# The taps of a depthwise convolution: VectorE alone, or shared with ScalarE and GpSimd

## The chip, the core and the metric

One core of a Trainium2 chip runs the whole program. The metric is device time in microseconds (us), the median over several executions. The engines are TensorE (PE for its matmuls, PEld for its weight loads), VectorE (DVE), ScalarE (ACT), GpSimd (POOL) and SyncE (SP, which issues DMAs). Each works through its own queue in order; semaphores tie the queues together.

## The reference

The program is a chain of three transformer-like blocks on x of 1024 positions by 1024 channels in float32. The change lies in the third block, whose input projection gives, among others, two halves of 512 channels for a gated convolution:

```python
def conformer_conv(glu_a, glu_b, dw_w, dw_b, cln_g, cln_b, pw_w, pw_b):
    u = glu_a * jax.nn.sigmoid(glu_b)
    pad = CONV_WIDTH // 2                       # CONV_WIDTH = 31
    u = lax.conv_general_dilated(
        u, dw_w[:, None, :].astype(u.dtype), window_strides=(1,),
        padding=[(pad, pad)], dimension_numbers=("NWC", "WIO", "NWC"),
        feature_group_count=u.shape[-1]) + dw_b
    u = layer_norm(u, cln_g, cln_b)
    u = jax.nn.silu(u)
    return u @ pw_w + pw_b
```

Each channel is convolved with its own 31 weights ("taps") along the 1024 positions. Beside this branch, the block computes a neighbourhood attention of 8 heads from the same projection. Both branches are normalised by groups, gated, joined and multiplied with w_out; a last norm gives the output.

## The kernel before

Activations lie with channels on the 128 partitions, so the 512 convolved channels are four tiles (i = 0 to 3) of 128 channels by 1024 positions. Each projection is a sum of matmuls in which every float32 operand is split into a rounded part "hi" and a remainder "lo": `weight` (lines 78 to 88) loads 128x1024 weights, makes `w_hi` on ScalarE or VectorE, and `w_lo` by a subtraction on GpSimd (line 87). Matmul results go to PSUM tiles of few buffers: `mm` has 2, `mf` has 1.

`block3` starts at line 1268. `glu(i)` (line 1283) makes the gated tile `u` of 128 x 1054 in a pool with two buffers for `u`; per half of 512 positions ScalarE takes a tanh (line 1290), and VectorE finishes the sigmoid (line 1291) and multiplies (line 1292). `dwconv(i, u)` (line 1297) then adds up 31 taps. Tap 0 is a multiply and add of the bias on VectorE (line 1304). Taps 1 to 20 are each one VectorE instruction, accumulator `cy` = `u` shifted by k, times a weight, plus `cy` (line 1306). Taps 21 to 30 go another way: ScalarE multiplies the shifted `u` by the weight, the first into `y2` (line 1308), the other nine one after the other into `pr`, a tile with one buffer (line 1311), and GpSimd adds each `pr` to `y2` (line 1312). The trace calls the tile `y2` "y". Last, VectorE adds `y2` to `cy` (line 1313) and SyncE stores `cy` to the DRAM tile `cv_d` (line 1314).

The order: convolutions 0 and 1 are emitted first (`convs`, lines 1425 to 1432). The attention runs in four pairs of heads, `na_pair(0)` to `na_pair(3)` (line 1370), each with projections split into `qs`, `ks`, `kl` (lines 144, 268, 273 and 279) and eight attention steps (`attend_steps`). One step goes PE scores, VectorE bias and maximum (line 329), ScalarE exponential (line 335), VectorE reciprocal and scaling (lines 337 and 341), PE transposes (line 346), ScalarE and VectorE split (lines 137 and 139), PE product (line 359), ScalarE copy (line 361), VectorE sum (line 366). `weave` (line 192) mixes other work between the steps: convolutions 2 and 3 and one gate projection in pair 0 (line 1437); `conv_ln` and `conv_pw` of one half in pair 1 and of the other in pair 2. `conv_ln` reads `cv_d` back (line 1321), transposes it (line 1324) and normalises it, so it needs all four convolutions.

The program is not run in the order in which it is written: the Tile layer's scheduler orders each engine's queue beforehand by its own timeline, in which an instruction that was emitted earlier goes first among those that are ready.

Of the kernel before, what the change touches and what calls it, by code (L numbers as in the profile page):

```python
# [10 lines left out]
F32 = mybir.dt.float32  # L11
F32R = mybir.dt.float32r
AF = mybir.ActivationFunctionType
ALU = mybir.AluOpType
# [4 lines left out]
P = 128  # L19
S = 1024  # L20
# [11 lines left out]
def kernel(ctx: ExitStack, tc: tile.TileContext, a, out, blocks=(1, 2, 3)):  # L32
    nc = tc.nc
    mm = nc.tensor.matmul
    act = nc.scalar.activation
    stt = nc.vector.scalar_tensor_tensor
    tt = nc.vector.tensor_tensor
    ts = nc.vector.tensor_scalar

    def pool(name, bufs=1, space=None, side=None, c=ctx):  # L40
        kw = {} if space is None else {"space": space}
        if side:
            kw["side"] = side
        if space is not DRAM:
            kw["reuse_waits"] = "tile"
        return c.enter_context(tc.tile_pool(name=name, bufs=bufs, **kw))
# [25 lines left out]
    def col(name, i, src=None):  # L72
        o = COL[name] + i
        return (cols if src is None else src)[:, o:o + 1]
# [1193 lines left out]
    def block3(x3, begin, finish):  # L1268
        x_st, x_fm = x3
        w3 = a["w_in_3"]  # L1270
        TAP, PAD = 31, 15
        POOL_TAPS = 10
        nc.scalar.dma_start(rpb_d.rearrange("r (b k) -> r b k", k=16),
                            bass.AP(tensor=a["rpb"].tensor, offset=a["rpb"].offset,
                                    ap=[[1, 16], [32, 248], [1, 16]]))
# [5 lines left out]
        cp = pool("conv", side="right", c=us)  # L1281
# [14 lines left out]

        def dwconv(i, u):
            y = cp.tile([P, S], F32, name="cy", tag="cy", bufs=2)
            y2 = cp.tile([P, S], F32, name="y2", tag="y2")
            for k in range(TAP):  # L1300
                w = col("dw_w_3", 4 * k + i)
                src = u[:, k:k + S]
                if k == 0:
                    ts(out=y, in0=src, scalar1=w, scalar2=col("dw_b_3", i), op0=ALU.mult, op1=ALU.add)
                elif k < TAP - POOL_TAPS:
                    stt(out=y, in0=src, scalar=w, in1=y, op0=ALU.mult, op1=ALU.add)  # L1306
                elif k == TAP - POOL_TAPS:
                    act(out=y2, in_=src, func=AF.Copy, scale=w)
                else:
                    pr = cp.tile([P, S], F32, name="pr", tag="pr", bufs=1)  # L1310
                    act(out=pr, in_=src, func=AF.Copy, scale=w)
                    nc.gpsimd.tensor_tensor(out=y2, in0=y2, in1=pr, op=ALU.add)
            tt(out=y, in0=y, in1=y2, op=ALU.add)
            nc.sync.dma_start(cv_d[i], y)

        def conv_ln(cp2, n_fm, hf):
# [104 lines left out]
        def conv_in(i):  # L1421
            u = yield from glu(i)
            dwconv(i, u)
# [85 lines left out]
    for b, body in ((1, block1), (2, block2), (3, block3)):  # L1509
        if b not in blocks:  # L1510
            continue
        n = b + 1 if b + 1 in blocks else 4
        if nxt is None:
            nxt = a["x"] if b == 1 else start(begin[b](), finish[b])
        nxt = body(nxt, begin[n], finish[n])
# [111 lines left out]
```

## Time and profile before

| | |
|---|---|
| Median of 3 runs | 3456.34 us (3452.67 to 3456.74) |
| The profiled execution, its own time | 3451.47 us |
| Its span, first to last instruction | 3449.7 us |
| Mean granted clock of TensorE | 0.971 |
| Third block's convolutions, taps on VectorE | 2828.8 to 3067 us of the span |

The page's first part gives the busy time of each engine. The chain of waits follows the work that ended last back through what released it. The window view gives busy time by engine for a stretch; the grouped view gives count, total and mean of like instructions; the timeline shows single instructions, where "x2" joins two neighbours and a bracket gives the idle time before one with its releaser. VectorE's instructions overlap by a few hundredths of a microsecond at their borders, so an instruction of 1.28 us takes 1.20 us from start to start.

### The profile page before, as it was taken

What the parts mean: (1) busy time and instruction counts of PE and PEld (TensorE: products, weight loads), DVE (VectorE), ACT (ScalarE), POOL (GpSimd) and SP (SyncE); (2) the same over time, 40 slices, a digit from 0 to 9 for tenths busy, and PEclk for the clock granted to TensorE, in tenths of its full rate; (3) what the DMA queues carried; (4) which work ended last, traced back from release to release, by engine and by line L of the source; (5) the groups of instructions that cost most, each with busy time, mean ns of one, the idle gap of its engine ahead of it and who ended that gap; (6) DMA issues with size and microseconds to landing.
All of it is one profiled execution on the core that took longest, in us unless ns stands there. A gap on an engine that the chain in (4) does not pass through costs nothing. (4 is left out here: it accounts for less than half of the span.)

```text
span 3449.7 us, 39897 instructions
## 1 busy us (share of the span) xinstructions
PE 3247.2 (94%) x14976; PEld 2658.2 (77%) x14976; DVE 2082.8 (60%) x3220; ACT 1102.8 (32%) x2038; POOL 1480.4 (43%) x949
## 2 busy tenths in 40 slices
PE   7999999999999999999978998999999986889998
PEld 6888888877888788778767776888888865667776
DVE  5455556374454455557768857444455679985665
ACT  3333311033223310311244532233321133445552
POOL 3111122266555642134434358555564456552221
PEclk9999999999999999999989999999999998989999
DMA  4211125212222432222251021222243221122241
GB/s 140 66 61 53 62 68 171 67 46 74 83 83 83 147 98 74 75 89 89 90 182 56 25 86 56 82 83 83 83 152 98 76 75 43 46 89 78 78 147 68
DMA packets 107474, 293.34 MB, mean 85 GB/s; under 512 B 15232, under 2 KB 20608, under 8 KB 107280
## 3 DMA queue, kind: packets, MB, share of 16 engines
q1 hardware_dynamic: 79184, 240.75, 21.4%
q10 hardware_dynamic: 28096, 50.04, 4.4%
q8 instruction: 118, 1.93, 0.2%
q14 instruction: 76, 0.62, 0.1%
HBM read 227.24 MB, written 63.76 MB: 84 GB/s over the span
## 5 line engine op out<-in xcount | busy, mean ns | idle before, releaser
L87 POOL TENSOR_TENSOR w_lo<-w_raw,w_hi 128x1024 fp32r<-128x1024 f32 x187 | 470.3, 2520 | 1042.4 <-DVE w_hi L86 569.2
L95 PE MATMUL mm<-x,w_hi 128*128 128x512 f32 x688 | 279.6, 407 | 22.9 <-DVE qs L144 10.8
L96 PE MATMUL mm<-x,w_hi 128*128 128x512 f32 x688 | 279.6, 406 | 0.0
L97 PE MATMUL mm<-x,w_lo 128*128 128x512 f32 x688 | 275.7, 402 | 1.0 <-POOL w_lo L87 1.0
L438 POOL TENSOR_TENSOR w_lo<-s,w_hi 128x512 fp32r<-128x512 f32 x160 | 220.2, 1384 | 103.9 <-ACT w_hi L437 102.5
L95 PE MATMUL mf<-x,w_hi 128*128 128x512 f32 x576 | 233.5, 405 | 17.9 <-DVE u L1292 13.9
L97 PE MATMUL mf<-x,w_lo 128*128 128x512 f32 x576 | 229.2, 398 | 1.2 <-POOL w_lo L87 1.2
L96 PE MATMUL mf<-x,w_hi 128*128 128x512 f32 x576 | 229.9, 399 | 0.0
L565 DVE TENSOR_TENSOR h<-h,mm 128x512 f32<-128x512 f32 x214 | 146.7, 687 | 134.7 <-PE mm L97 134.6
L438 POOL TENSOR_TENSOR w_lo<-w_raw,w_hi 128x512 fp32r<-128x512 f32 x120 | 172.1, 1434 | 97.7 <-ACT w_hi L437 97.4
L86 DVE CAST w_hi<-w_raw 128x1024 fp32r<-128x1024 f32 x143 | 134.9, 944 | 128.3 <-PE mm L96 58.6
L519 DVE TENSOR_TENSOR u<-p,pb 128x512 f32<-128x512 f32 x40 | 27.5, 687 | 248.6 <-PE pb L97 248.6
L95 PEld LDWEIGHTS mm<-x,w_hi 128*128 128x128 f32 x688 | 132.6, 193 | 55.7 <-issue 23.4
L437 ACT CAST w_hi<-s 128x512 fp32r<-128x512 f32 x160 | 97.2, 619 | 243.3 <-PE pc L96 148.6
L1306 DVE SCALAR_TENSOR_TENSOR cy<-u,cols,cy 128x1024 f32<-128x1024 f32 x80 | 166.2, 2084 | 0.9
L97 PEld LDWEIGHTS mm<-x,w_lo 128*128 128x128 f32 x688 | 132.5, 193 | 30.4 <-issue 2.2
L96 PEld LDWEIGHTS mm<-x,w_hi 128*128 128x128 f32 x688 | 133.1, 193 | 27.4 <-issue 2.1
L335 ACT ACTIVATE st<-st,nmax 128x128 f32<-128x128 f32 (+5 forms) x192 | 119.3, 623 | 107.2 <-DVE nmax L329 101.4
L95 PE MATMUL mm<-w_hi,act 128*128 128x512 f32 x384 | 150.5, 392 | 2.9 <-DVE h L565 2.9
L96 PE MATMUL mm<-w_lo,act 128*128 128x512 f32 x384 | 150.5, 392 | 0.3 <-POOL w_lo L87 0.3
L97 PE MATMUL mm<-w_hi,act 128*128 128x512 f32 x384 | 150.3, 392 | 0.0
L95 PEld LDWEIGHTS mf<-x,w_hi 128*128 128x128 f32 x576 | 110.7, 192 | 42.2 <-DVE u L1292 15.0
(505 smaller groups left out, 9017.4 us busy)
## 6 DMA issues: line engine op xcount, KB each, us to landing
w_raw<-in_w_ffn_in_dram SPq DMA_DIRECT2D x88, 512.0 KB, 3.6
w_raw<-in_w_in_dram SPq DMA_DIRECT2D x78, 512.0 KB, 3.7
act_d<-ao SPq DMA_DIRECT2D x88, 256.0 KB, 2.0
w_raw<-in_w_ffn_out_dram SPq DMA_DIRECT2D x44, 512.0 KB, 3.9
act<-act_d SPq DMA_DIRECT2D x36, 512.0 KB, 4.3
w_raw<-in_w_out_dram SPq DMA_DIRECT2D x24, 512.0 KB, 3.7
gates_d<-go SPq DMA_DIRECT2D x32, 256.0 KB, 2.0
gt<-gates_d ACTq DMA_DIRECT2D x32, 256.0 KB, 3.4
```

Source lines behind the costliest of these rows:

```text
L86: nc.vector.tensor_copy(hi, raw)
L87: nc.gpsimd.tensor_tensor(out=lo, in0=raw, in1=f(hi), op=ALU.subtract)
L95: mm(out_, lh, rh, start=start and i == 0, stop=False, **kw)
L96: mm(out_, lh, rl, start=False, stop=False, **kw)
L97: mm(out_, ll, rh, start=False, stop=stop and i == n - 1, **kw)
L335: act(out=st[:, :w + extra], in_=st[:, :w + extra], func=AF.Exp, scale=-1.0, bias=nmax, accum_out=ssum)
L437: nc.scalar.copy(hi, src)
L438: eng(out=lo, in0=src, in1=f(hi), op=ALU.subtract)
L519: tt(out=u3, in0=p1, in1=pb, op=ALU.add)
L565: tt(out=hh, in0=hh, in1=pt, op=ALU.add)
L1306: stt(out=y, in0=src, scalar=w, in1=y, op0=ALU.mult, op1=ALU.add)
```

## The change

All 31 taps are computed by VectorE's multiply-add of line 1306. The ten ScalarE multiplications of a tile, the nine GpSimd additions, the closing VectorE addition and the tiles `y2` and `pr` are gone. Everything else in the program text is the same; the scheduler orders the queues anew.

```diff
-        POOL_TAPS = 10
...
         def dwconv(i, u):
             y = cp.tile([P, S], F32, name="cy", tag="cy", bufs=2)
-            y2 = cp.tile([P, S], F32, name="y2", tag="y2")
             for k in range(TAP):
                 w = col("dw_w_3", 4 * k + i)
                 src = u[:, k:k + S]
                 if k == 0:
                     ts(out=y, in0=src, scalar1=w, scalar2=col("dw_b_3", i), op0=ALU.mult, op1=ALU.add)
-                elif k < TAP - POOL_TAPS:
+                else:
                     stt(out=y, in0=src, scalar=w, in1=y, op0=ALU.mult, op1=ALU.add)
-                elif k == TAP - POOL_TAPS:
-                    act(out=y2, in_=src, func=AF.Copy, scale=w)
-                else:
-                    pr = cp.tile([P, S], F32, name="pr", tag="pr", bufs=1)
-                    act(out=pr, in_=src, func=AF.Copy, scale=w)
-                    nc.gpsimd.tensor_tensor(out=y2, in0=y2, in1=pr, op=ALU.add)
-            tt(out=y, in0=y, in1=y2, op=ALU.add)
             nc.sync.dma_start(cv_d[i], y)
```

## Rows read from the trace of the kernel before

**Rows 1.** Page: busy us of each engine, share of the span, instructions

```profile
PE 3247.2 (94%) x14976; PEld 2658.2 (77%) x14976; DVE 2082.8 (60%) x3220; ACT 1102.8 (32%) x2038; POOL 1480.4 (43%) x949
```

**Rows 2.** Windows: stretch, its us, busy us of each engine, granted clock, DMA

```profile
2828.80:3067.00 238.20, 190.69 (x789) 147.04 (x788) 236.48 (x227) 95.37 (x143) 142.60 (x59) 0.88 0.15 45
3067.00:3092.00 25.00, 19.93 (x77) 15.03 (x76) 17.93 (x22) 11.51 (x21) 14.78 (x6) 0.80 0.30 95
3092.00:3449.70 357.70, 330.01 (x1467) 255.31 (x1465) 210.65 (x445) 169.20 (x330) 75.85 (x49) 0.95 0.28 97
```

**Rows 3.** Chain of waits, 2828 to 3092 us: start, us, what (its longest pieces)

```profile
2943.39 3.32 DVE cy L1306
2947.04 3.33 DVE cy L1306
...
3070.59 4.64 DVE gr L1260 x2
3076.16 4.21 DVE st L341 x2
```

**Rows 4.** Timeline of DVE, 2896 to 2917 us: start, us, instruction, idle before

```profile
2898.60 1.28 DVE L1306 SCALAR_TENSOR_TENSOR cy<-u,cols,cy 128x1024 f32<-128x1024 f32 x1
...
2904.18 6.42 DVE L1306 SCALAR_TENSOR_TENSOR cy<-u,cols,cy 128x1024 f32<-128x1024 f32 x2
2910.53 0.15 DVE L337 RECIPROCAL ssum<-ssum 128x1 f32<-128x1 f32 x1
2910.64 3.24 DVE L1306 SCALAR_TENSOR_TENSOR cy<-u,cols,cy 128x1024 f32<-128x1024 f32 x1
```

**Rows 5.** Timeline of POOL, 2896 to 2917 us

```profile
2897.12 0.11 POOL L1287 MEMSET u<- 128x15 f32 x1
2903.87 2.37 POOL L1312 TENSOR_TENSOR y<-y,pr 128x1024 f32<-128x1024 f32 x1 [6.63 <-ACT y L1308]
2906.20 3.33 POOL L87 TENSOR_TENSOR w_lo<-w_raw,w_hi 128x1024 fp32r<-128x1024 f32 x1
2909.49 3.31 POOL L1312 TENSOR_TENSOR y<-y,pr 128x1024 f32<-128x1024 f32 x1
```

**Rows 6.** Groups of DVE by shape, 2828 to 3092 us: count, busy us, mean ns, idle before

```profile
L1306 DVE SCALAR_TENSOR_TENSOR cy<-u,cols,cy 128x1024 f32<-128x1024 f32 x80 | 166.2, 2084 | 0.9
L341 DVE TENSOR_SCALAR st<-st,ssum 128x384 f32<-128x384 f32 x15 | 15.6, 1058 | 0.0
...
L1313 DVE TENSOR_TENSOR cy<-cy,y 128x1024 f32<-128x1024 f32 x4 | 6.7, 1682 | 0.0
L1304 DVE TENSOR_SCALAR cy<-u,cols 128x1024 f32<-128x1024 f32 x4 | 6.7, 1667 | 0.1
...
L1291 DVE TENSOR_SCALAR sg<-sg 128x512 f32<-128x512 f32 x5 | 6.0, 1193 | 0.0
...
L1260 DVE SCALAR_TENSOR_TENSOR gr<-aT,half,gr 128x512 f32<-128x512 f32 x2 | 4.7, 2398 | 0.0
L1292 DVE SCALAR_TENSOR_TENSOR u<-mf,cols,sg 128x512 f32<-128x512 f32 x6 | 4.5, 742 | 4.0 <-PE mf L97 4.0
```

**Rows 7.** By line and by tile: shortest/median/longest ns, first and last start

```profile
L1304 DVE TENSOR_SCALAR cy<-u,cols x4: 1003/1334/2998, 2828.8 to 3002.3; 128x1024 f32<-128x1024 f32 x4
L1313 DVE TENSOR_TENSOR cy<-cy,y x4: 1212/1216/3084, 2901.4 to 3088.7; 128x1024 f32<-128x1024 f32 x4
L341 DVE TENSOR_SCALAR st<-st,ssum x20: 336/407/2543, 2901.1 to 3077.9; 128x384 f32<-128x384 f32 x15, 128x256 f32<-128x256 f32 x5
L1291 DVE TENSOR_SCALAR sg<-sg x5: 414/415/2596, 2852.7 to 2982.9; 128x512 f32<-128x512 f32 x5
```

**Rows 8.** Groups of POOL and ACT by shape, 2828 to 3092 us

```profile
L1312 POOL TENSOR_TENSOR y<-y,pr 128x1024 f32<-128x1024 f32 x36 | 98.0, 2722 | 64.9 <-ACT pr L1311 44.1 <-ACT y L1308 13.7 <-DVE ssum L337 5.7
L87 POOL TENSOR_TENSOR w_lo<-w_raw,w_hi 128x1024 fp32r<-128x1024 f32 x16 | 45.1, 2816 | 32.2 <-ACT w_hi L84 12.0 <-issue 10.5 <-PE tr L346 5.9
...
L1264 POOL TENSOR_TENSOR gr<-gr,z 128x1024 f32<-128x1024 f32 x1 | 2.4, 2357 | 0.7 <-issue 0.7
L1311 ACT ACTIVATE pr<-u,cols 128x1024 f32<-128x1024 f32 x36 | 41.4, 1149 | 33.2 <-POOL y L1312 28.8 <-DVE ssum L337 4.3
```

**Rows 9.** Timeline of all engines, 3065 to 3100 us: the fourth convolution's end

```profile
3065.70 1.27 DVE L1306 SCALAR_TENSOR_TENSOR cy<-u,cols,cy 128x1024 f32<-128x1024 f32 x1
...
3088.70 3.08 DVE L1313 TENSOR_TENSOR cy<-cy,y 128x1024 f32<-128x1024 f32 x1
...
3099.24 0.60 PE L1324 MATMUL mf<-sq_c,cv 128*128 128x128 f32 x4
```

## The prediction

> **What bounds the kernel now.** I read the page's busy line first, then the windows around the third block's convolutions, then the chain of waits inside that stretch, and last the single instructions of VectorE and GpSimd side by side.
>
> Over the span TensorE is the busy engine, with 94% against VectorE's 60% [rows 1]. That is a mean over stages. From 2828.8 us, where the first tap starts, to 3067 us, where the last one ends, VectorE is busy 236.5 of 238.2 us, while TensorE is busy 190.7 us at a granted clock of 0.88 [rows 2]. So in this stretch VectorE is the bound, and TensorE has 47 us of idle time in it. After 3092 us it is the other way round: TensorE 330 of 358 us, VectorE 59% [rows 2]. The chain of waits agrees: its longest pieces between 2828 and 3092 us are VectorE's, taps of 3.3 us among them [rows 3].
>
> A tap of 3.3 us is the odd thing. The timeline shows the same instruction at 1.28 us while GpSimd is idle, between 2897.2 and 2903.9 us, and then at 6.42 us for two and 3.24 us for one as soon as GpSimd runs its 128x1024 subtractions and additions back to back [rows 4, 5]. GpSimd pays as well, 3.3 us instead of 2.37 [rows 5]. The two seem to take turns: a tap that meets a GpSimd instruction waits for about 2.1 us of it. So the mean tap takes 2.084 us [rows 6], and much of VectorE's "busy" time is waiting for GpSimd.
>
> **What the waiting costs.** I sum what each kind of VectorE instruction takes above its undisturbed duration between 2828 and 3092 us. Taps: 80 x (2.084 - 1.28) = 64.3 us [rows 4, 6]. Scaling of scores, line 341: 15 x (1.058 - 0.407) = 9.8 [rows 6, 7]. Line 1291: 5 x (1.193 - 0.415) = 3.9. Line 1304: 4 x (1.667 - 1.003) = 2.7. Line 1313: 4 x (1.682 - 1.212) = 1.9. Line 1260: two at 2.398, for which I take the 0.742 of line 1292's like shape [rows 6], 3.3. Together 85.9 us. GpSimd's full-size instructions in the same stretch are 36 additions, 16 `w_lo` and one of line 1264, 53 in all [rows 8], so one of them costs VectorE 1.62 us on average. I leave out GpSimd's small casts of line 273; the single pairs that I looked at show little from them.
>
> **The change part by part.**
> - Removed, 36 GpSimd additions: 36 x 1.62 = 58.3 us of VectorE waiting. Bounds: if all 17 other GpSimd instructions cost the whole 2.1 us, 85.9 - 35.7 = 50.2 us are left for the additions; if every addition costs 2.1 us, 75.6 us. I take the mean, since the additions are of the same shape as `w_lo` and come between the same taps.
> - Removed, four closing additions (line 1313): 4 x 1.2 = 4.8 us of VectorE (their waiting is counted above) [rows 7].
> - Removed, 40 ScalarE multiplications: 40 x 1.15 = 46 us of ScalarE, which is busy 95 of 238 us [rows 2, 8]. ScalarE is not the bound and the value is nothing, though the 28.8 us in which its queue stood before a `pr` [rows 8] also go. What came behind those waits on ScalarE met a full VectorE.
> - Added, 40 taps on VectorE at 1.20 us from start to start: 48.0 us (51.2 at 1.28).
> - Left as they are, 17 GpSimd instructions. They still cost 1.62 us each, at worst 2.1, which would be 8 us more. GpSimd is no longer late, so each starts as soon as its inputs are there, and about as many of VectorE's instructions can meet it.
> - The fourth convolution's end. Its taps end at 3067 us, but GpSimd's lane trails, the closing addition starts at 3088.7, and the first transposes of the result run at 3099.2 [rows 9]. Now the store would follow the last tap. I give this nothing: TensorE is busy 20 of 25 us there [rows 2], so at most 5 us are to be had, and part of them is the waiting of lines 1260 and 341, already in the sum. If the last tap came later instead, what is late next is the normalisation of the convolution, with 30 us of room before it is where it is today.
> - Tiles, queues and DMAs: `u` comes free for convolutions 2 and 3 with the last VectorE tap, no longer with ScalarE's last read. No DMA is added; SyncE's store waits for one engine less. Nothing.
>
> Sum: -58.3 - 4.8 + 48.0 = -15.1 us of VectorE work, of which 10 lie before 3067 us and 5 behind. VectorE is the bound there and TensorE has the room, so I let it all count: span 3449.7 - 15.1 = 3434.6. The profiled execution took 1.8 us more than its span, giving 3436.4, and lies 4.9 us below the median of the runs, so the median becomes 3441. Of the bounds: -50.2 - 4.8 + 51.2 + 8 = +4 us, and -75.6 - 4.8 + 48 = -32 us.
>
> **The rivals.**
> 1. *No change.* Both unkind bounds hold: the additions cost only 1.4 us each and the remaining `w_lo` cost the full 2.1. The sum is then about zero, 3456. For it: the margin per tile is small, ten taps at 1.2 less one closing addition (10.8 us) against nine additions at 1.62 (14.6). Against it: an addition follows its predecessor within 1.3 us or less in rows like those shown, so it nearly always meets a tap.
> 2. *Slower: VectorE doesn't stay full.* Its waiting fills time in which it would else have waited for attention. Without it, VectorE's own work between 2828.8 and 3067 is some 159 us (236.5 less 77 of the 85.9). After the change it is 159 + 48 - 3.6 = 204 us, and with 14 `w_lo` at 1.62 about 226. The stage gets longer if VectorE is busy less than 226/238 = 95% of it. At 90%, 251 us, 13 more: 3469. For it: behind this stage VectorE idles 41% of the time [rows 2], since each attention step goes back and forth between four engines, and the scheduler sets a new order. Against it: taps need only the tap before, and 0.9 us of idle time stands before all 80 of them [rows 6].
> 3. *More than forecast.* Every addition costs the whole 2.1 us: -32 us, 3424. For it: rows like 3.24 and 3.32. Against it: the mean is 1.62.
> 4. *Much slower.* The waiting isn't the additions' doing and stays: 48 - 4.8 = 43 us more on a full engine, 3500. Against it are rows 4 and 5.
>
> [...]
>
> **How the numbers follow.** A measurement of this kernel can tell about 0.2%, 7 us, from no change: faster is below 3449.4, slower above 3463.3. Forecast (3428 to 3449): 0.45. No change: 0.23. VectorE not full: 0.21. Whole turns: 0.08. Much slower: 0.03. So faster 0.53, same 0.23, slower 0.24. The forecast's own range is 3428 to 3449; the range to hold 8 times in 10 runs from whole turns, 3422, to just beyond the 90% case, 3470.
>
> **What the profile after would show.** Line 1306 has 120 taps with a mean near 1.28 + 17 x 1.62/120 or so, 1.4 to 1.55 us, and long ones only beside a `w_lo`; lines 1308, 1311, 1312 and 1313 are gone. From the first tap to the last, about 228 us with VectorE busy 97% or more. The first transposes of line 1324 stand closer behind the last tap than 32 us. TensorE's granted clock there rises a little from 0.88, and behind the stage all is as before but earlier. I am wrong if taps stay near 2 us (rival 4), if VectorE shows idle time waiting for ScalarE or TensorE between taps (rival 2), or if a later stage gives back what this one saves.

## The result, and the profile after

The changed kernel takes 3420.3 us (median of five, 3418.3 to 3423.9) where the kernel before takes 3456.7 (five, 3452.7 to 3461.6): a ratio of 0.9894, 95% interval 0.988 to 0.9909. It is 36 us faster. The direction was forecast; the size was not: 15 us were forecast, and 3420.3 lies just under the range, which began at 3422.

The two profiled executions show a little less, a span of 3420.8 after 3449.7, or 28.9 us; the one of before lay 5 us below its median, the one of after 2 us above its own.

The page after, busy us of each engine over the span (the counterpart of rows 1):

```profile
PE 3239.9 (95%) x14976; PEld 2655.8 (78%) x14976; DVE 2073.7 (61%) x3256; ACT 1059.6 (31%) x1998; POOL 1383.7 (40%) x913
```

VectorE has 36 instructions more and is busy 9 us less. So three times as much time was gained as VectorE was busy less. That is what has to be explained.

The window view after, from the first tap to the last and from there to the end (rows 2; columns: us, then busy us of PE, PEld, DVE, ACT, POOL, granted clock, DMA share, GB/s):

```profile
2824.40:3077.30 252.90, 228.20 (x986) 179.65 (x985) 250.58 (x306) 70.18 (x138) 64.02 (x30) 0.93 0.18 60
3077.30:3420.80 343.50, 310.04 (x1345) 238.75 (x1343) 203.54 (x425) 162.93 (x315) 73.98 (x48) 0.92 0.27 95
```

VectorE is still full, 250.6 of 252.9 us, and the last tap comes later than before (3077 for 3067), although the program ends earlier. The taps themselves, as groups by shape and by shortest, median and longest ns (rows 6 and 7):

```profile
L1304 DVE SCALAR_TENSOR_TENSOR cy<-u,cols,cy 128x1024 f32<-128x1024 f32 x120 | 180.6, 1524 | 0.9
L341 DVE TENSOR_SCALAR st<-st,ssum 128x384 f32<-128x384 f32 x18 | 7.1, 404 | 0.0
L1302 DVE TENSOR_SCALAR cy<-u,cols 128x1024 f32<-128x1024 f32 x4 | 3.2, 800 | 0.1
```

```profile
L1304 DVE SCALAR_TENSOR_TENSOR cy<-u,cols,cy x120: 1252/1275/3432, 2825.3 to 3076.1; 128x1024 f32<-128x1024 f32 x120
```

The mean tap fell from 2.084 to 1.524 us, the scaling of line 341 from 1.058 to 0.404. One of the long taps that remain, in the timelines of POOL and DVE after (rows 4 and 5): it starts while a `w_lo` is under way and ends 1.1 us after it, about as an undisturbed tap (1.2 us from start to start) would that had been let in when the `w_lo` ended.

```profile
2920.04 2.38 POOL L87 TENSOR_TENSOR w_lo<-w_raw,w_hi 128x1024 fp32r<-128x1024 f32 x1 [11.39 <-ACT w_hi L84]
```

```profile
2920.84 2.67 DVE L1304 SCALAR_TENSOR_TENSOR cy<-u,cols,cy 128x1024 f32<-128x1024 f32 x1
```

**Where the 28.9 us lie.** Both traces are divided at two cuts: the start of the first tap, and the start of pair 2's first `qs` on ScalarE, behind which both do the same work. The stretch between the cuts, before and then after:

```profile
2828.80:3172.20 343.40, 287.23 (x1212) 222.56 (x1211) 295.77 (x351) 146.44 (x248) 171.52 (x74) 0.88 0.19 59
```

```profile
2824.40:3142.70 318.30, 281.86 (x1215) 221.10 (x1214) 284.81 (x386) 102.76 (x207) 75.95 (x38) 0.90 0.19 64
```

The stretch is 25.1 us shorter. TensorE runs the same matmuls in both (1212 and 1215 recorded); it is idle 56.2 us before and 36.4 after, 19.7 less, and busy 5.4 us less, at a granted clock of 0.90 where it was 0.88. Ahead of the first tap the changed kernel is 4.4 us earlier, behind the second cut 0.6 us slower (278.1 for 277.5 us): 19.7 + 5.4 + 4.4 - 0.6 = 28.9. Seen from VectorE, the 25.1 us are 11.0 us less busy time (295.8 and 284.8) and 14.1 us less idle time (47.6 and 33.5).

**Why TensorE idles less.** The stretch divided at the end of pair 0's first attention step and at the end of its last, before and after:

```profile
2828.80:2938.20 109.40, 81.19 (x325) 63.55 (x324) 108.42 (x82) 40.74 (x54) 68.34 (x28) 0.84 0.13 39
2938.20:3043.80 105.60, 89.00 (x385) 68.75 (x384) 105.00 (x128) 44.11 (x77) 60.94 (x28) 0.90 0.17 54
3043.80:3172.20 128.40, 117.04 (x506) 90.26 (x505) 82.35 (x143) 61.59 (x119) 42.24 (x19) 0.89 0.26 81
```

```profile
2824.40:2902.10 77.70, 64.06 (x264) 50.05 (x262) 76.91 (x74) 19.49 (x32) 22.68 (x10) 0.89 0.13 41
2902.10:3007.40 105.30, 94.37 (x406) 74.96 (x407) 103.99 (x144) 26.15 (x59) 23.95 (x14) 0.91 0.17 54
3007.40:3142.70 135.30, 123.43 (x547) 96.09 (x546) 103.92 (x170) 57.12 (x117) 29.32 (x15) 0.91 0.25 85
```

By length all of the gain is in the first piece, 31.7 us; the second is as long as before and the third 7 us longer. But the changed kernel also has 61 matmuls fewer in the first piece (264 for 325) and runs them later, so a fairer measure is TensorE's idle time: it falls from 28.2 to 13.6 us in the first piece, from 16.6 to 10.9 in the second, and is 11.4 and 11.9 in the third. Of the 19.7 us, 14.6 lie in the first piece and 5.7 in the second. The groups of VectorE say why. Taps ahead of the first step's end, before and after:

```profile
L1306 DVE SCALAR_TENSOR_TENSOR cy<-u,cols,cy 128x1024 f32<-128x1024 f32 x40 | 86.3, 2169 | 0.6
```

```profile
L1304 DVE SCALAR_TENSOR_TENSOR cy<-u,cols,cy 128x1024 f32<-128x1024 f32 x42 | 65.1, 1577 | 0.5
```

The additions beside the taps of the first of these groups:

```profile
L1312 POOL TENSOR_TENSOR y<-y,pr 128x1024 f32<-128x1024 f32 x14 | 39.9, 2853 | 22.4 <-ACT pr L1311 14.5 <-ACT y L1308 6.6 <-DVE cy L1306 1.1
```

The scheduler puts as many taps ahead of the first step as before (40 and 42, with the tap-0 instructions 43 and 44), and they take 21 us less, because 14 of the 36 GpSimd additions stood beside them. The added taps, on the other hand, come later: the second piece holds 46 in place of 31 and the third 33 in place of 9. In the first two pieces VectorE is full before and after (idle 1.6 us of 215, and 2.1 of 183). In the third it was idle for 46.1 us and is now for 31.4, so the taps there are in part hidden in time that VectorE had to spare. How much, the run with 21 taps below shows: of 50.6 us more VectorE work, 9.1 fit into its idle time. The saving was taken where VectorE is full; most of the added work was paid for as well, but not all of it.

### The profile page after: what moved, and what is told of

It reads as the page before. It is cut to its first block, busy times and chain, and to the rows that moved or that the text cites. A ratio compares the mean times of both kernels' runs of the same rounds, so it can differ in the third digit from the quotient of the medians.

```text
span 3420.8 us, 39879 instructions
## 1 busy us (share of the span) xinstructions
PE 3239.9 (95%) x14976; PEld 2655.8 (78%) x14976; DVE 2073.7 (61%) x3256; ACT 1059.6 (31%) x1998; POOL 1383.7 (40%) x913
## 5 line engine op out<-in xcount | busy, mean ns | idle before, releaser
L95 PE MATMUL mm<-x,w_hi 128*128 128x512 f32 x688 | 276.5, 402 | 13.0 <-DVE kl L279 8.0
L96 PE MATMUL mm<-x,w_hi 128*128 128x512 f32 x688 | 273.9, 398 | 0.0
L1304 DVE SCALAR_TENSOR_TENSOR cy<-u,cols,cy 128x1024 f32<-128x1024 f32 x120 | 180.6, 1524 | 0.9
L137 ACT ACTIVATE pth<-tr 128x512 fp32r<-128x512 f32 (+3 forms) x224 | 95.8, 451 | 148.6 <-PE tr L346 108.2
```

The costliest lines, as they stand in the source:

```text
L95: mm(out_, lh, rh, start=start and i == 0, stop=False, **kw)
L96: mm(out_, lh, rl, start=False, stop=False, **kw)
L137: act(out=hi, in_=src, func=AF.Copy, scale=scale)
```

## The experiments

Each run is compared with the kernel before on the same chip. "The lane" is the way of taps 21 to 30 over ScalarE's multiplications and GpSimd's additions. In the listings of the runs that keep lane instructions the tap's line is 1305 or 1306. The expectations set three causes against each other: A, turns (GpSimd's additions hold VectorE), B, order (only the scheduler's new order matters) and C, the freed ScalarE. The table has the runs from which the terms of the sum are taken.

| Run | Additions on GpSimd | Lane on ScalarE | Taps on VectorE, of 31 | Median us | Ratio to before (95%) |
|---|---|---|---|---|---|
| kernel before | yes | yes | 21 | 3456 | 1 |
| e4 | no | yes | 21 | 3393.6 | 0.9822 (0.9807 to 0.9836) |
| e10 | no | no | 21 | 3383.2 | 0.979 (0.9774 to 0.9807) |
| e1 | yes | yes | 31 | 3499.1 | 1.0124 (1.0107 to 1.0141) |
| e2 | no | yes | 31 | 3430.4 | 0.9926 (0.9911 to 0.9941) |
| changed kernel, again | no | no | 31 | 3422.4 | 0.9901 (0.9886 to 0.9916) |

**The changed kernel with the old lane beside it (e1).** ScalarE's multiplications and GpSimd's additions run as before; their sum is not used.

```diff
+                if k == TAP - 10:
+                    act(out=y2, in_=src, func=AF.Copy, scale=w)
+                elif k > TAP - 10:
+                    pr = cp.tile([P, S], F32, name="pr", tag="pr", bufs=1)
+                    act(out=pr, in_=src, func=AF.Copy, scale=w)
+                    nc.gpsimd.tensor_tensor(out=y2, in0=y2, in1=pr, op=ALU.add)
```

> The changed kernel (31 taps on VectorE), with the old lane of ten ScalarE multiplications and nine GpSimd additions per tile kept beside it; its result y2 is used by nobody, so the output is the same. Theory A, taking turns: each GpSimd addition makes a VectorE instruction wait, and it is this waiting that left. Then 36 x 1.6 = 58 us of VectorE waiting come back on top of all 124 tap instructions, some two thirds of them ahead of attention's instructions: 3455 to 3480 us. Theory B, order: the gain is the scheduler's new order of the queues, in which more taps stand behind attention; the order here is near that of the changed kernel, so 3420 +- 8. Theory C, ScalarE: the gain is ScalarE's queue, freed of 40 multiplications that waited for GpSimd: 3435 to 3456.

Measured: 3499.1 us, 43 more than before, and 19 above the highest figure of any of the three. The window between the same two cuts:

```profile
2826.80:3216.50 389.70, 297.87 (x1214) 230.13 (x1213) 346.68 (x386) 145.47 (x246) 183.31 (x74) 0.82 0.17 52
```

TensorE idles 91.8 us there, at a granted clock of 0.82. This kernel has forty taps more than the one before and four closing additions fewer. So while GpSimd's additions stay, forty taps less four closing additions cost 43 us, and the gain of the change is not the work of a new order alone (B forecast 3420).

**The changed kernel with ScalarE's part of the lane alone (e2).** As above without the line that adds.

> The changed kernel with only the 40 ScalarE multiplications of the old lane beside it (results unused, output the same), no GpSimd additions. A: ScalarE takes no turns with VectorE, 3420 +- 8. B: the scheduler orders anew once more, so any value within some 15 us of 3420. C: 46 us of ScalarE come back in front of attention's exponentials, 3430 to 3445.

Measured: 3430.4 us. Against the run before, the 36 additions alone are worth 69 us with 31 taps on VectorE; against the changed kernel (3420 to 3422), forty unused multiplications on ScalarE cost 8 to 10 us. That is above the range of A (up to 3428) and at the low end of C's; B's 15 us either way don't rule it out.

**The kernel before without its additions (e4).** Nine of the 31 taps are left out of each tile's result.

```diff
-                    nc.gpsimd.tensor_tensor(out=y2, in0=y2, in1=pr, op=ALU.add)
```

> The kernel before with its 36 GpSimd additions left out: taps 22 to 30 are multiplied on ScalarE and thrown away, so the convolution lacks nine taps. It takes the waiting away and adds no tap. A: the mean tap falls from 2.08 to about 1.5 us, VectorE has 58 us less, more than TensorE's idle time there (47 us): 3405 to 3422 us, with VectorE no longer full. B: no more than order moves it, 3440 to 3465. C: ScalarE no longer waits for GpSimd but still multiplies: 3435 to 3450.

Measured: 3393.6 us, 62 less than before and 11 under A's range. The window between the cuts:

```profile
2828.10:3110.10 282.00, 263.36 (x1201) 208.72 (x1201) 233.55 (x348) 143.86 (x243) 72.17 (x38) 0.96 0.22 72
```

The same matmuls, with TensorE idle 18.6 us and a granted clock of 0.96. The additions alone cost 62 us with 21 taps. The forecast had 58.3 for them. VectorE's busy time fell by 62.2 us between the cuts and the stretch by 61.4, so what went counted in full.

**The lane with a write in place of the addition (e3).** GpSimd overwrites `pr` with zeros instead of adding it.

```diff
-                    nc.gpsimd.tensor_tensor(out=y2, in0=y2, in1=pr, op=ALU.add)
+                    nc.gpsimd.memset(pr, 0.0)
```

> As the kernel with the whole lane beside it, but each GpSimd addition is replaced by a GpSimd memset of the same 128x1024 tile, which reads nothing (output the same). A in its narrow form, only a GpSimd instruction that reads SBUF holds up a tap: taps beside a memset take 1.28 us, 3420 +- 8. A in its wide form, any GpSimd instruction does: taps of more than 2 us beside memsets, 3435 or more. B: 3420 +- 8 with no change of a tap's duration expected. C: 3430 to 3445.

Measured: 3431.1 us, as with no GpSimd addition there (3430.4), and so by ScalarE's 10 us above what A in its narrow form forecast from the changed kernel. The groups of DVE and of POOL, 2824 to 3090 us:

```profile
L1305 DVE SCALAR_TENSOR_TENSOR cy<-u,cols,cy 128x1024 f32<-128x1024 f32 x120 | 169.5, 1430 | 1.0
```

```profile
L1311 POOL MEMSET pr<- 128x1024 f32 x36 | 34.4, 955 | 43.2 <-ACT pr L1310 43.2
```

36 GpSimd instructions that only write leave the taps at 1.43 us, no longer than the 1.48 without them. Side by side in the timelines, 26 taps ran while a memset and no other GpSimd instruction was under way: they took 1.276 us on average and 1.287 at most, and the 62 taps with nothing beside them 1.273 on average. Five taps in a row from 2946.18 us took 6.16 us, 1.22 from start to start, with memsets starting at 2946.78, 2948.98 and 2951.18. So GpSimd does not hold a tap by being busy alone: its memsets, which read nothing, left the taps at 1.28 us, while in the kernel before a tap beside one addition, which reads two tiles, took 3.41 (at 2872.89 us).

**Half of the lane (e5).**

```diff
-        POOL_TAPS = 10
+        POOL_TAPS = 5
```

> The kernel before with 5 instead of 10 taps on ScalarE and GpSimd: 16 GpSimd additions instead of 36, 100 taps on VectorE instead of 80. A, taking turns: parts go by count, -62 x 20/36 for the additions, +37 x 20/40 for the taps, -5 for ScalarE: 3430 to 3442, about half of the change. B, order: no fixed relation to the count, anything from 3415 to 3460.

Measured: 3431.9 us (0.9936, 0.9919 to 0.9954), between the two kernels and inside A's range; B's was too wide to be tested by it. With 16 additions for 36 the mean tap is 1.66 us.

**The `w_lo` of this stage on VectorE (e6).** The GpSimd subtractions of line 87 that are emitted with the convolutions go to VectorE.

```diff
-        nc.gpsimd.tensor_tensor(out=lo, in0=raw, in1=f(hi), op=ALU.subtract)
+        lo_eng[0].tensor_tensor(out=lo, in0=raw, in1=f(hi), op=ALU.subtract)
```

> The changed kernel, and while the convolutions run (weights of convolutions 0 to 3, pairs 0's and the first gate's) the remainder w_lo is subtracted on VectorE instead of GpSimd. A: of the 18 w_lo that still hold VectorE up, those moved cost 1.2 us on VectorE instead of 1.78 us of waiting, so 12 of them give 7 us less VectorE work: 3408 to 3418. Rival: a w_lo stands in VectorE's queue behind taps, TensorE waits for it: 3422 to 3435.

Measured: 3423.8 us (0.9908, 0.989 to 0.9925), no different from the changed kernel, where 3408 to 3418 had been expected of twelve moved subtractions. Seven moved, and each takes 1.22 us on VectorE. The mean tap fell from 1.524 to 1.416 us, which is 12.9 us in all or 1.85 for each that moved. The seven would thus save 4 us, which the interval does not resolve.

**ScalarE's lane cut to 8 columns (e8).** As the run with ScalarE's part alone, each multiplication on 8 of 1024 columns.

> The changed kernel with the 40 ScalarE multiplications of the old lane beside it, but each on 8 columns instead of 1024 (results unused, output the same). The full-size ones cost 10 us over the changed kernel. If it is ScalarE's time (46 us) that costs them, the small ones (about 40 x 0.2 = 8 us) cost 0 to 3 us: 3419 to 3424. If it is only the scheduler's other order, or that 40 more instructions stand in ScalarE's queue, they cost the same: 3427 to 3433.

Measured: 3425.8 us (0.9914, 0.9896 to 0.9933), between the two ranges; the interval touches both neighbours, so how the 10 us divide between ScalarE's time and its queue is not settled by it.

**ScalarE's lane that reads its own tile (e14).** Nine of ten multiplications read `y2` in place of `u`.

> The changed kernel with forty more ScalarE multiplications, nine of each ten reading the tile that the first one wrote and not the convolved input; their result is unused. The run in which all forty read the input took 3430 us, the one with forty of 8 columns 3426, the changed kernel 3420 to 3422. If the lane's price is ScalarE's time: 3428 to 3432. If it is that the lane holds the input tile until its last read, so that the next convolution's gate is written later: 3420 to 3426.

Measured: 3433.8 us (0.9935, 0.9918 to 0.9953). It is 11 to 13 us above the changed kernel. So the multiplications cost their 10 us though nine of ten don't hold `u`.

**The changed kernel with 21 taps (e10).** Taps 21 to 30 are left out of the result, and the lane is gone too. The changed kernel itself was measured again beside it (e11).

```diff
-            for k in range(TAP):
+            for k in range(TAP - 10):
```

> The changed kernel with taps 0 to 20 alone; taps 21 to 30 are left out of the result. The lane on ScalarE is gone as well, so against the run without additions (3394 us, which kept the ScalarE multiplications and the closing addition) this shows what that lane costs when VectorE has only 20 taps a tile, and against the changed kernel what ten more taps a tile cost. If ScalarE's lane is worth 10 us wherever it stands: 3384, and the 40 taps cost 36. If the lane is hidden with 20 taps: 3394 less up to 5 us for the closing additions, 3389 to 3394, and the 40 taps cost 26 to 31. If every tap counted in full (40 x 1.20 = 48 us): 3372.

> The changed kernel, unaltered, beside the three others of this group, so that they can be set against it directly: 3420 us, within 5.

Measured: 3383.2 and 3422.4 us. Ten taps more in a tile cost 39.1 us in all, not the 48 of 40 x 1.20. Against the 3393.6 above, ScalarE's lane and the closing additions together are worth 10.4 us. The window of the 21 taps between the cuts:

```profile
2823.40:3100.20 276.80, 265.21 (x1211) 210.34 (x1210) 234.20 (x348) 101.30 (x207) 72.32 (x39) 0.98 0.23 74
```

TensorE idles 11.6 us. To the changed kernel that is 24.9 us of idle time and 16.7 us of slower matmuls: two fifths of what forty taps cost between the cuts is slower matmuls (granted clock 0.98 with 21 taps, 0.90 with 31).

VectorE's side says why 48 us of taps did not cost 48. Its busy time rises by 50.6 us from this kernel to the changed one (234.2 to 284.8), the stretch by 41.5 (276.8 to 318.3), and its idle time falls by 9.1 (42.6 to 33.5). Of the 9.1, 7.2 lie behind pair 0's last step, where this kernel has 8 taps and the changed one 33:

```profile
2990.60:3100.20 109.60, 107.71 (x509) 84.75 (x509) 71.02 (x142) 54.48 (x113) 25.29 (x14) 0.98 0.29 95
```

Even there a tap is not cheap: TensorE idles 1.9 us in that piece, and 11.9 in the changed kernel's.

**All taps ahead of the attention (e9).** All four convolutions are emitted before pair 0.

```diff
         lane[0] = "mf"
         for c_ in convs:
             for _ in c_:
                 pass
+        for i in (2, 3):
+            for _ in conv_in(i):
+                pass
...
-        weave(p0, ("mf", [(conv_in(2), 2), (conv_in(3), 2), (zgate(np_, 4), 2)], 7))
+        weave(p0, ("mf", [(zgate(np_, 4), 2)], 7))
```

> The changed kernel with all four convolutions emitted ahead of the attention's first pair; only the gate projection is left to be mixed in. The same instructions, another place. If it matters where the taps stand against the attention (taps ahead of pair 0's last step count in full, those behind it slide under TensorE's work): about 33 taps more in front, 50 us, of which some 20 us are given back in pair 0 itself, so 3440 to 3475. If only the sum of VectorE's work counts: 3420, within 8.

Measured: 3450.8 us (0.9985, 0.9976 to 0.9994), 28 more than the changed kernel with the same instructions; the profiled execution is the slowest of its ten, 3456.8. The window from its first tap to its last, and what PE waited for up to pair 0's end (in total, times, longest):

```profile
2828.10:3043.50 215.40, 153.02 (x605) 117.01 (x606) 212.24 (x231) 41.30 (x81) 39.35 (x20) 0.81 0.14 43
```

```profile
PE mf L95 <- DVE u L1291: 44.7, 3, 37.2
PE sp L323 <- DVE nmax L329: 7.8, 5, 2.9
```

The taps run faster than in the changed kernel (215 us for all, 253 there), and yet TensorE is idle 62 of these 215 us, waiting for VectorE to reach the next `u`. Place counts, and not the sum of VectorE's work alone.

**Fewer taps ahead of the attention (e15).** Only convolution 0 is emitted ahead of pair 0, the other three between its steps.

```diff
-        convs = [conv_in(i) for i in range(2)]
+        convs = [conv_in(i) for i in range(1)]
...
-        weave(p0, ("mf", [(conv_in(2), 2), (conv_in(3), 2), (zgate(np_, 4), 2)], 7))
+        weave(p0, ("mf", [(conv_in(1), 2), (conv_in(2), 2), (conv_in(3), 2), (zgate(np_, 4), 2)], 7))
```

> The changed kernel with only convolution 0 emitted ahead of pair 0, and 1, 2 and 3 mixed in between its steps. If taps ahead of pair 0's last step count and those behind it slide, this can move up to 31 more taps, 37 us of VectorE, behind it; behind it there is room for about 30 us more before the convolution's normalisation is late. Gain 0 to 15 us, 3405 to 3420. If the fourth convolution then ends so late that the normalisation is waited for, as in the run that moved convolution 3 to pair 1: 3425 to 3445.

Measured: 3422.9 us (0.9903, 0.9887 to 0.992), the same as the changed kernel. The window between the cuts:

```profile
2828.90:3144.70 315.80, 279.53 (x1207) 217.55 (x1206) 278.53 (x384) 98.88 (x203) 72.19 (x37) 0.92 0.20 63
```

Pair 0 ends 138.8 us after the first tap, not 183, and TensorE's idle time is still 36.3 us. VectorE is busy 98% from the first tap to the last, which again takes 252.6 us (252.9 in the changed kernel). TensorE's idle time up to the last tap falls from 24.7 to 20.5 us, and behind it, up to the second cut, it rises from 11.7 to 15.8. So of the gain in front nothing was left. That taps behind pair 0 are cheaper only until they make the convolution's end late fits this, but this one run does not show that it is the reason.

**The fourth convolution beside pair 1 (e7).** Convolution 3 moves into pair 1, and the normalisation and projection of both halves into pair 2.

```diff
-        weave(p0, ("mf", [(conv_in(2), 2), (conv_in(3), 2), (zgate(np_, 4), 2)], 7))
+        weave(p0, ("mf", [(conv_in(2), 2), (zgate(np_, 4), 2), (zgate(np_, 5), 2)], 7))
+        p1 = na_pair(1)
+        next(p1)
+        weave(p1, ("mf", [(conv_in(3), 2)], 4), ("mm", [(zgate(np_, i), 2) for i in (0, 1, 2, 3)], 8))
```

> The changed kernel with convolution 3 woven into attention pair 1 instead of pair 0, and conv_ln and conv_pw of both halves into pair 2; two gate projections come earlier as filler. A: 31 taps (37 us of VectorE) leave the stretch where VectorE is full and TensorE idles 24 us and go to one where TensorE is the bound: TensorE's idle time up to pair 0's end halves, 3400 to 3415. Rival: pair 2 now has all the normalisation, with chains between four engines and less filler, and gives it back: 3420 to 3440.

Measured: 3441.2 us (0.996, 0.9947 to 0.9974), 21 more than the changed kernel. The waits of PE from 3105 us, where pair 2 begins, to the end (in total, times, longest):

```profile
PE mm L1320 <- DVE xn L784: 16.5, 4, 8.2
PE tr L346 <- DVE st L341: 6.8, 4, 3.3
```

This lies 1 us above the rival's range. The stretch to pair 2 is 40 us shorter than in the changed kernel and the rest 60 us longer. Part of that is work that moved (110 matmuls more in the rest), but TensorE's idle time is 10 us less in the first part and 29 us more in the rest, where the longest wait is for the convolution's normalisation (`xn`).

**The scaling of the scores on ScalarE, pairs 0 and 1 (e12, e13).** The first of two runs also took one buffer from the second block's attention and lost 14 us before the first tap, so it tells nothing; the second has that buffer back (`deep` is true in the second block alone) and is the one shown.

```diff
-                st = pl.tile([P, smax + extra], F32, name="st", tag="st", bufs=3 if act_norm is not None else 2)
+                st = pl.tile([P, smax + extra], F32, name="st", tag="st", bufs=3 if deep else 2)
...
-                                        bias_of, lambda t: (max(0, t - 1), min(NT, t + 2)), dst_of, smax=384, rev=True)
+                                        bias_of, lambda t: (max(0, t - 1), min(NT, t + 2)), dst_of, smax=384, rev=True,
+                                        act_norm=(lambda z, u: True) if hp < 2 else None)
```

> The changed kernel with the scaling of the scores (line 341) on ScalarE for the first two pairs of heads, 16 of the 384 or 256 wide instructions, some 0.4 us each and more beside GpSimd. If VectorE is still what bounds pair 0 after the change: 5 to 10 us faster, 3410 to 3415. If pair 0 is bound by the chain of its steps from engine to engine, where ScalarE takes longer for the same instruction: 3420 to 3430.

> As the run before with the scaling of the scores of the first two pairs on ScalarE, but with the second block's buffers left as they were, so that only the third block differs. If VectorE's sum of work bounds pair 0 after the change: 5 to 10 us under the changed kernel, 3411 to 3416. If the chain of steps from engine to engine binds, or what pair 0 gains is given back behind it: 3417 to 3425.

Measured: 3436.1, and without the fault 3422.1 us (0.9905, 0.9887 to 0.9922), the same as the changed kernel. Pair 0 ends 17 us earlier after the first tap (166.0 for 183.0), and pair 2 begins where it did (316.9 for 318.3). What was gained inside pair 0 was given back behind it.

No version beat the changed kernel with the whole result computed.

## Why the prediction was wrong in size

**What bounds the kernel.** Right: VectorE is full through the stretch before and after, and 0.9 us of idle time stands before all 120 taps, as before the 80 [rows 6]. What was missed is that "full" does not make each of its microseconds count.

**The waiting for GpSimd.** Right in mechanism and nearly in size: 58.3 us forecast, 62 measured with 21 taps and 69 with 31. The GpSimd instructions that remain cost what was taken: the 120 taps stand 29.3 us above 1.28 us each, by 18 full-size instructions 1.63, for the 1.62 of the forecast. The forecast's mean could not show that 14 of the 36 additions stood where VectorE holds the attention's start.

**The forty taps.** The term was mis-sized: 48 us, measured 39 without the lane. (With the lane kept, forty taps less the four closing additions cost 43; with the forecast's 4.8 for the closing additions, nothing of the 48 is hidden there.) Of the forty, 2 came into the piece ahead of pair 0's first step, 15 between its steps and 24 behind it (by the counts of the groups, which take a tap at a border twice), where VectorE had idle time to spare. Against the run with 21 taps 9.1 us of idle time were filled, 7.2 of them behind that last step.

**ScalarE and the closing additions.** This step failed: 4.8 us for the closing additions and nothing for ScalarE, where the runs give 10.4 together, and 8 to 10 for ScalarE's multiplications alone. The reason given, that what came behind ScalarE's waits met a full VectorE, does not make it nothing. Where in the trace the 10 us lie stays open in the main: between the cuts the run with ScalarE's lane differs from the changed kernel by 2.7 us, ahead of the first tap by 4.0, behind by 0.7; with 21 taps, with and without the lane and closing additions, it is 5.2, 4.7 and 0.7. About 1.9 us of the part ahead of the first tap come with the lane in every trace (see the last paragraph of this section). Beyond that the start of the first tap moves from one execution to the next (2824.4 and 2825.9 us in two of the changed kernel, 2823.4 to 2832.9 over all runs that left the second block alone), with and without the lane.

The terms as the runs give them, each against its neighbour: -62 (additions), -10 (ScalarE's lane and closing additions), +39 (taps), together -33 for the measured -34 to -36. The forecast had -58.3, -4.8 and +48: about 4, 6 and 9 us off, all on the same side.

**"I let it all count".** This is the step behind the taps' error. It took the sum of VectorE's work, -15.1 us, for the change of the time. VectorE's busy time fell by 9.1 us in fact, and the time by 29 in the same two executions; the rest is idle time of VectorE that went. The run with all taps first has VectorE 2 us less busy still and loses 28 us. And the clock was named among the signs ("rises a little from 0.88") but had no term: it is 5.4 of the 25.1 us between the cuts.

**The fourth convolution's end.** Right that it need not matter: the last tap is 10 us later, as the step allowed for, and the store follows it at once. DVE's last taps, SP's store and PE's first transposes of the result after (rows 9):

```profile
3074.77 2.58 DVE L1304 SCALAR_TENSOR_TENSOR cy<-u,cols,cy 128x1024 f32<-128x1024 f32 x2
```

```profile
3077.38 0.32 SPq L1305 DMA_DIRECT2D cv_d<-cy  x1
```

```profile
3083.52 0.60 PE L1315 MATMUL mf<-sq_c,cv 128*128 128x128 f32 x4
```

The transposes run 6 us behind the last tap, not 32, and 16 us earlier than before.

**The rivals.** "No change" did not come: the additions cost 1.7 to 1.9 us of time each, not 1.4. The argument against it, that an addition follows its predecessor within 1.3 us, took too few rows for the whole: 64.9 us of idle time before 36 additions [rows 8] are 1.8 us each. "VectorE doesn't stay full" did not come: 99%. It is what moving convolution 3 to pair 1 does (272 of 307 us). "Whole turns" named nearly the right time, 3424, for the wrong reason: the whole gain would have been in the additions. "The waiting stays" is refuted by the 62 and 69 us.

**The signs.** The mean tap of 1.4 to 1.55 us came (1.524), and so did VectorE above 97%, the transposes close behind the last tap, and a later part that is as before. "About 228 us from the first tap to the last" did not: 252.9. The stretch took in attention work that stood behind the last tap in the kernel before, as the later taps let it pass: 986 matmuls ran in it, 789 before.

**The range.** Its low end, 3422, was one term at its bound, with the others as forecast. Three terms that each erred by less than 10 us to the same side go past it.

**The 4.4 us ahead of the first tap** are in part an effect of the change. From 2790 to 2815 us TensorE is 1.9 us busier after, at the same granted clock; before and then after:

```profile
2790.00:2815.00 25.00, 22.21 (x111) 17.82 (x110) 11.93 (x18) 7.62 (x12) 6.84 (x8) 1.00 0.26 88
```

```profile
2790.00:2815.00 25.00, 24.06 (x119) 19.71 (x118) 13.38 (x17) 7.28 (x12) 6.00 (x4) 1.00 0.26 81
```

Most of it is one wait of 1.3 us for line 1290's `sg`. It stands in the traces of all eight kernels that keep lane instructions, the one with 8 columns too, and in neither trace of the changed kernel:

```profile
PE mf L95 <- ACT sg L1290: 1.3, 1, 1.3
```

The rest I could not tie to the change. TensorE stands idle 9.9 us there in both kernels and its 128x512 matmuls then start 0.43 us apart for a while (granted clock from 2767 to 2790 us: 0.63 before, 0.70 after): before, they still do at 2788.5 us and start 0.23 apart from 2789.4; after, the last pair 0.43 apart is here:

```profile
2785.36 0.63 PE L97 MATMUL mf<-x,w_lo 128*128 128x512 f32 x1
2785.79 0.44 PE L95 MATMUL mf<-x,w_hi 128*128 128x512 f32 x1
2786.07 0.40 PE L96 MATMUL mf<-x,w_hi 128*128 128x512 f32 x1
```

In the second execution of the changed kernel they start 0.43 us apart until 2788.8 us (granted 0.63), so this part belongs to the execution.

## What to carry to other kernels

Removing work from a full engine is worth what the engines that wait for it gain at the place where it stood: ask which instructions of the bottleneck's queue stand ahead of the engine that sets the end, and price the removed and the added work by that, not by one sum for the stage. Ten multiply-adds of 1.2 us on VectorE were cheaper here than nine additions on a GpSimd that is else busy a quarter of the stretch (64 of 253 us), because each addition cost 1.7 to 1.9 us of time (62 and 69 us by 36), and ScalarE's multiplications another 8 to 10 us in all. When TensorE's idle time changes, give its clock a term of its own: between the cuts it was granted 0.82 with 91.8 us of idle time (e1) and 0.98 with 11.6 (e10).

## What the runs showed of the hardware that was not expected

The same 1210 or so matmuls between the cuts took 297.9, 287.2, 281.9 and 265.2 us as TensorE's idle time among them went from 91.8 over 56.2 and 36.4 to 11.6 us and the granted clock from 0.82 over 0.88 and 0.90 to 0.98. Over these four runs each microsecond more of idle time goes with about 0.4 us of slower matmuls ((297.9 - 265.2) / (91.8 - 11.6)). The four kernels also differ in order and in VectorE's work, so this is what went together in them and no price that holds elsewhere.

A GpSimd memset of 128x1024, 0.955 us (e3), left VectorE's two-input taps at 1.28 us, while additions of the same shape lengthened them to as much as 3.4 (the kernel before). Forty multiplications on ScalarE (e2), which was busy less than half of the stretch (146 of 321 us) and whose results nobody read, cost 8 to 10 us.
